# Cross attention of eight short streams in fp32, four samples side by side in four column groups of TensorE

## The chip, the cores and the metric

The kernel runs on one core of one Trainium2 chip. The metric is the device time of one execution in microseconds (us); lower is better. Engines are named as in the profile: PE is the matrix engine (PEld its weight loads), DVE, ACT and POOL are the vector, scalar and GpSimd engines, SP issues most of the DMA transfers from one queue that works strictly in order.

## The reference

One layer of a streaming encoder is computed for two groups of rows: 2048 rows of one new stream ("prompt", 16 tiles of 128 rows) and 128 rows that belong to eight running streams of 16 rows each ("samples", one tile, `S_TILE`). The change concerns the attention of the samples, in two places. Cut to these:

```python
# 1. mixer attention: the 16 rows of a sample attend to 256 cached rows and their own 16, 8 heads of 64
s = einsum("bqhd,bkhd->bhqk", q, k) * 64 ** -0.5 + bias;  att = softmax(s) @ v
y = concat(att, conv_branch) @ w_out;   x = x + rmsnorm(y) * g
# 2. cross attention: the same 16 rows attend to 256 memory rows of that sample, 4 heads of 256
q = (rmsnorm(x) @ w_mq).reshape(B, T, 4, 256)
s = einsum("bthd,bmhd->bhtm", q, mk) * 256 ** -0.5      # mk, mv = cache_mem_k, cache_mem_v
o = einsum("bhtm,bmhd->bthd", softmax(s), mv).reshape(B, T, 1024)
x = x + rmsnorm(o @ w_mo) * g
```

The caches `cache_att_k`, `cache_att_v`, `cache_mem_k` and `cache_mem_v` are inputs of the layer. A function `layout` on the host reorders inputs into the arrays that the kernel reads.

## The kernel before, in words

Stages follow one another: memory keys of the prompt, input projection and convolution (to about 640 us), band attention (`attention`, 640 to 920 us), output projection (`mixout`, 920 to 1190 us), cross attention of the prompt (`phase_cross`), the gated feed-forward layer (`gate_up`) and its down projection (`down`). Dense products use a three-product split: each fp32 operand is taken as a high and a low part in a reduced format that PE reads in one pass (tiles `sbr`, `sbx` hold these), and `mm3` / `mm3h` (lines 283 to 291) multiply high by high, high by low, low by high. A few products are left in plain fp32; the trace shows one of these as two records.

`attention` runs 128 units (8 heads by 16 row tiles), and in each head the eight-step generator `sample(s)` is woven in for one sample. It loads 256 cached keys with the key index on the partitions (`kc`, 512 KB), turns them with eight transposes on PE (line 812) through PSUM and two ACT copies (line 813) into `kt` (channel on the partitions), adds the 16 new keys (POOL, line 816), and makes the scores with four fp32 products of 32 weight columns each (line 826). Each of the four writes its own 32 rows of PSUM, that is, its own quarter of the columns of PE; in `kt` 272 columns pass. Line 845 does the same with the values.

`mixout` multiplies 17 row tiles (the samples' first) with `w_out`: 48 products of 512 columns for each (line 291). From the third tile on, after each second of the eight k-steps, `RATE` steps of the generator `cross_sample` are woven in; what is left runs after the last tile. `cross_sample` does the samples' cross attention: the query product (`dense`), 16 steps of scores, softmax, 16 steps of values, the output product (`dense`). A step of scores takes half of one sample's keys: eight transposes (line 1175), a split into high and low by ACT (1177) and DVE (1178), then eight products of 256 columns with 128 weight columns (line 1194), in which only the 16 columns of that sample are not zero; hence the two zeroed tiles `pads`, which POOL fills with a sample's 16 columns and blanks again (line 1130). A step of values splits a loaded block and has eight such products (line 1231). Cached blocks of 512 KB come into three buffers `wf`, one SP transfer each (line 1096).

The order in which each engine's instructions stand is fixed when the program is built: a scheduler places the generators' instructions by its own estimate of when they can run. So a change of steps also changes the order around them. Tile memory is laid out by hand in `Region`; a load into a buffer waits until the buffer's last reader is done.

Of the kernel before, what the change touches and what calls it, by code (L numbers as in the profile page):

```python
# [8 lines left out]
F32 = mybir.dt.float32  # L9
F32R = mybir.dt.float32r  # L10
# [24 lines left out]
RATE = 1.0  # L35
# [101 lines left out]
class Build:  # L137
# [611 lines left out]
    def att_pools(self):  # L749
        sbF, sbR, fa, fb = self.sbF, self.sbR, self.fa, self.fb  # L750
        self.attp = (Region().lay(sbF, 34.5, ("kc", 4, 2), ("kt", 4.25, 1), ("pp", 1.5, 1), ("vn", 2, 1))
# [31 lines left out]
    def attention(self):  # L783
# [14 lines left out]
        def sample(s):  # L798
            kc = self.t(pool, [P, 2, 512], F32, "kc", 2)
            nc.sync.dma_start(kc[:, :, :], A["cache_att_k"][s].rearrange("(b p) d -> p b d", p=P))  # L800
# [5 lines left out]
            kt = self.t(pool, [P, 4, PAST + DEC_S], F32, "kt", 1)  # L806
            for c2 in range(0, 4, 2):
                pt = self.t(ps_t, [P, 2, 2, P], F32, "t")
                for c in range(2):
                    for b in range(2):  # L810
                        cc = slice((c2 + c) * P, (c2 + c + 1) * P)
                        nc.tensor.transpose(pt[:, c, b, :], kc[:, b, cc], self.ident[:, :])
                nc.scalar.copy(kt[:, c2:c2 + 2, :PAST].rearrange("p c (b k) -> p c b k", k=P), pt[:, :, :, :])
                if c2 == 0:
                    yield
# [173 lines left out]
    def mixout(self, ctx):  # L989
        nc, A = self.nc, self.A  # L990
        sbF, sbR = self.sbF, self.sbR
        fr, ff = self.flex(ctx, (4096, F32R)), self.fa
# [7 lines left out]
                .at("kvh", 4, (sbR, [64, 80]), (fr, [8])).at("kvl", 4, (sbR, [68, 104]), (fr, [12])))  # L1000
# [73 lines left out]
    def cross_sample(self, pool, ps_so, ps_p):  # L1074
# [7 lines left out]
        pads = [self.t(pool, [P, KC, P], F32R, f"pad{i}", 1) for i in range(2)]  # L1082
        for pd in pads:
            nc.gpsimd.memset(pd[:, :, :].bitcast(F32), 0.0)
            yield
# [13 lines left out]
        def transposed(src, dst, scale=1.0):  # L1099
            th = self.t(pool, [P, KC, P], F32R, "sTh", 1)  # L1100
            tl = self.t(pool, [P, KC, P], F32R, "sTl", 1)
            for half in range(2):
                sl = slice(4 * half, 4 * half + 4)
                pt = self.t(ps_p, [P, 4, P], F32, "p")
                for k in range(4):
                    nc.tensor.transpose(pt[:, k, :], src(4 * half + k), self.ident[:, :])
                nc.scalar.activation(th[:, sl, :], pt[:, :, :], AF.Copy, scale=scale)
                nc.vector.scalar_tensor_tensor(tl[:, sl, :], pt[:, :, :], scale, th[:, sl, :].bitcast(F32),
                                               ALU.mult, ALU.subtract)
                yield  # L1110
            dst += [th, tl]

        def dense(lhs, wn, y):
            ahead = Ahead([lambda k=k: split(load(A[wn][k])[:, :]) for k in range(KC)])
# [6 lines left out]
        def places(s):  # L1121


            own = s * DEC_S
            other = (own + 64) % P
            return [slice(o, o + DEC_S) for o in (own, other)]

        def blank(s):
            for c in places(s):
                nc.gpsimd.memset(pads[s % 2][:, :, c].bitcast(F32), 0.0)  # L1130

        def pad(s, T):
            if s >= 2:
                blank(s - 2)
            for c, src in zip(places(s), T):
                nc.gpsimd.tensor_copy(pads[s % 2][:, :, c], src[:, :, s * DEC_S:(s + 1) * DEC_S])
            return pads[s % 2]

        def clear():
            for s in (DEC_B - 2, DEC_B - 1):  # L1140
                blank(s)

        def gather(dst, src, g):

            own, other = slice(g * 64, g * 64 + 64), slice(64 - g * 64, P - g * 64)
            nc.scalar.copy(dst[own], src[other])
            nc.vector.tensor_tensor(dst[own], dst[own], src[own], ALU.add)
# [9 lines left out]
        nc.scalar.activation(q[:, :], flat(y), AF.Copy, scale=1.0 / 16.0)  # L1157
# [549 lines left out]
```

## Time and profile before

| | |
|---|---|
| time, median of 3 runs | 3013.76 us (3012.63 to 3015.66) |
| the profiled execution's own time | 3012.76 us |
| its span in the trace | 3011.0 us |
| PE busy | 97% of the span, 16932 products |
| DVE, ACT, POOL busy | 71%, 45%, 46% |
| mean DMA rate | 166 GB/s |

The span is what the trace covers; 1.8 us of the execution lie around it. Rows of the profile's timeline read: start in us from the span's start, length in us, engine, line, what is written from what, shape, how many. Lengths of products overlap, since PE works on the next before the last has left it; the cost of a row in a busy stretch is therefore the distance from its start to the next row's start.

### The profile page before, as it was taken

What the parts mean: (1) busy time and instruction counts of PE and PEld (TensorE: products, weight loads), DVE (VectorE), ACT (ScalarE), POOL (GpSimd) and SP (SyncE); (2) the same over time, 40 slices, a digit from 0 to 9 for tenths busy, and PEclk for the clock granted to TensorE, in tenths of its full rate; (3) what the DMA queues carried; (4) which work ended last, traced back from release to release, by engine and by line L of the source; (5) the groups of instructions that cost most, each with busy time, mean ns of one, the idle gap of its engine ahead of it and who ended that gap; (6) DMA issues with size and microseconds to landing.
All of it is one profiled execution on the core that took longest, in us unless ns stands there. A gap on an engine that the chain in (4) does not pass through costs nothing.

```text
span 3011.0 us, 46007 instructions
## 1 busy us (share of the span) xinstructions
PE 2925.7 (97%) x16932; PEld 2676.2 (89%) x16932; DVE 2126.8 (71%) x3077; ACT 1354.8 (45%) x2726; POOL 1392.6 (46%) x1304
## 2 busy tenths in 40 slices
PE   8999999979999999999999999999999999999998
PEld 8999999968887887787888999999999999888786
DVE  6696895958885466435358888888788998556655
ACT  4545464658883344323234333433344444433433
POOL 0267495710013235235357565546555776424413
PEclk9999999989999999999999999999999999999999
DMA  8635255557744556324246333544334446756664
GB/s 305 241 112 183 92 162 161 170 153 184 191 132 164 176 194 212 109 75 137 95 151 227 119 136 117 200 156 152 133 136 157 140 144 208 253 174 209 224 198 164
DMA packets 196430, 500.09 MB, mean 166 GB/s; under 512 B 18981, under 2 KB 82989, under 8 KB 187875
## 3 DMA queue, kind: packets, MB, share of 16 engines
q1 hardware_dynamic: 185883, 461.09, 47.8%
q0 software_dynamic: 10320, 36.05, 3.1%
q8 instruction: 133, 2.18, 0.3%
q14 instruction: 94, 0.77, 0.1%
HBM read 365.97 MB, written 141.81 MB: 169 GB/s over the span
## 4 chain that ended last, share of the span: by engine, by line
PE 38%; DMA 4%; POOL 3%; issue 3%; DVE 2%; ACT 1%; SPq 0%; DVEq 0%; POOLq 0%; ACTq 0%
PE psb L285 12%; PE psb L284 12%; PE psb L283 12%; DMA sbf<-in_w_down_dram 2%; POOL sbf L1558 1%; PE psb L291 1%; DMA sbf<-x 1%; PE psb L1413 1%; DVE sbr L1619 0%; POOL sbf L340 0%; DVE sbr L1436 0%; DMA sbf<-in_w_gate_dram 0%; DMA sbf<-hn 0%; DMA hn<-sbf 0%; DVE flexb L1498 0%
## 5 line engine op out<-in xcount | busy, mean ns | idle before, releaser
L283 PE MATMUL psb<-sbr 128*128 128x384 f32 (+3 forms) x2808 | 944.3, 338 | 3.5 <-ACT sbr L319 1.1
L284 PE MATMUL psb<-sbr 128*128 128x384 f32 (+3 forms) x2356 | 807.6, 343 | 2.6 <-DVE sbr L320 2.4
L285 PE MATMUL psb<-sbr 128*128 128x512 f32 (+3 forms) x1848 | 634.3, 345 | 3.7 <-DVE sbr L1619 3.5
L283 PEld LDWEIGHTS psb<-sbr 128*128 128x128 f32 x2808 | 531.4, 190 | 33.5 <-ACT sbr L1618 2.4
L285 PE MATMUL psb<-sbr,sbx 128*128 128x384 f32 (+2 forms) x1484 | 478.3, 323 | 0.1
L284 PEld LDWEIGHTS psb<-sbr 128*128 128x128 f32 x2356 | 446.1, 189 | 29.2 <-DVE sbr L320 2.7
L285 PEld LDWEIGHTS psb<-sbr 128*128 128x128 f32 x1848 | 348.4, 189 | 33.4 <-DVE sbr L1619 6.9
L291 PE MATMUL psb<-sbr 128*128 128x512 f32 x1200 | 297.8, 397 | 4.3 <-POOL sbr L1271 1.5
L1436 DVE TENSOR_TENSOR sbr<-sbf,sbr 128x512 fp32r<-128x512 f32 x258 | 262.6, 1021 | 39.8 <-ACT sbr L1435 38.9
L1435 ACT CAST sbr<-sbf 128x512 fp32r<-128x512 f32 x258 | 159.3, 620 | 276.5 <-PE psb L284 234.6
L285 PEld LDWEIGHTS psb<-sbr,sbx 128*128 128x128 f32 x1484 | 281.4, 190 | 0.6 <-POOL sbx L278 0.4
L523 DVE SCALAR_TENSOR_TENSOR psb<-sbf,psb 128x768 f32<-128x768 f32 (+1 forms) x290 | 264.4, 912 | 6.2
L291 PEld LDWEIGHTS psb<-sbr 128*128 128x128 f32 x1200 | 223.6, 190 | 50.5 <-POOL sbr L1271 1.9
L1619 DVE TENSOR_TENSOR sbr<-sbf,sbr 128x384 fp32r<-128x384 f32 (+1 forms) x231 | 166.5, 743 | 92.6 <-ACT sbr L1618 91.3
L278 POOL TENSOR_TENSOR sbx<-sbf,sbr 128x1024 fp32r<-128x1024 f32 x60 | 152.9, 2551 | 81.3 <-ACT sbr L277 77.7
L1558 POOL TENSOR_TENSOR sbf<-sbf 128x512 f32<-128x512 f32 x77 | 107.6, 1401 | 167.9 <-DMA sbf<-in_w_down_dram 166.2
L1618 ACT CAST sbr<-sbf 128x384 fp32r<-128x384 f32 (+1 forms) x231 | 110.5, 497 | 164.9 <-PE psb L284 133.4
L533 POOL TENSOR_TENSOR flexb<-flexb,flexb 128x128 f32<-128x128 f32 (+1 forms) x180 | 167.1, 929 | 21.7 <-ACT flexb L532 12.1
L283 PE MATMUL psb<-sbr,sbx 128*128 128x384 f32 (+1 forms) x524 | 170.8, 327 | 2.5 <-ACT sbx L1435 1.8
L1435 ACT CAST sbx<-sbf 128x512 fp32r<-128x512 f32 x153 | 94.7, 620 | 163.4 <-PE psb L284 143.2
L1436 DVE TENSOR_TENSOR sbx<-sbf,sbx 128x512 fp32r<-128x512 f32 x153 | 154.5, 1012 | 17.9 <-ACT sbx L1435 17.5
L277 ACT CAST sbr<-sbf 128x1024 fp32r<-128x1024 f32 x98 | 102.5, 1050 | 108.2 <-PE psb L284 56.1
(339 smaller groups left out, 6159.7 us busy)
## 6 DMA issues: line engine op xcount, KB each, us to landing
af<-flexb SPq DMA_DIRECT2D x33, 1344.0 KB, 6.1
sbf<-in_w_down_dram SPq DMA_DIRECT2D x154, 256.0 KB, 3.8
sbf<-af SPq DMA_DIRECT2D x90, 384.0 KB, 3.9
sbf<-in_w_gate_dram SPq DMA_DIRECT2D x66, 512.0 KB, 3.4
sbf<-in_w_up_dram SPq DMA_DIRECT2D x66, 512.0 KB, 3.5
sbf<-x SPq DMA_DIRECT2D x49, 512.0 KB, 4.0
sbf<-in_w_in_dram SPq DMA_DIRECT2D x48, 512.0 KB, 4.2
sbr<-ks SPq DMA_DIRECT2D x28, 512.0 KB, 10.3
```

Source lines behind the costliest of these rows:

```text
L278: self.lo_engine.tensor_tensor(lo[:, :], wf[:, :], hi[:, :].bitcast(F32), ALU.subtract)
L283: nc.tensor.matmul(ps, lh, rh, start=start, stop=False, **kw)
L284: nc.tensor.matmul(ps, lh, rl, start=False, stop=False, **kw)
L285: nc.tensor.matmul(ps, ll, rh, start=False, stop=stop, **kw)
L291: nc.tensor.matmul(y[o], l, r[:, o * 512:(o + 1) * 512], start=start and x == 0, stop=stop and x == 2)
L523: nc.vector.scalar_tensor_tensor(acc if w < CW - 1 else o, src(w), cwt[:, j, w:w + 1], acc, ALU.mult, ALU.add)
L533: nc.gpsimd.tensor_tensor(o, o, v, ALU.add)
L1435: nc.scalar.copy(hs[j][:, :], src[j])
L1436: nc.vector.tensor_tensor(ls[j][:, :], src[j], hs[j][:, :].bitcast(F32), ALU.subtract)
L1558: nc.gpsimd.tensor_tensor(acc[:, :], acc[:, :], q[:, :], ALU.add if s > 0 else ALU.subtract)
L1618: nc.scalar.copy(ch[:, m], a[:, x, m])
L1619: nc.vector.tensor_tensor(cl[:, m], a[:, x, m], ch[:, m].bitcast(F32), ALU.subtract)
```

## The change

The host stores the cached keys with the channel first: `cache_att_kt` (per sample, channel by key) and `cache_mem_kt`, and `cache_mem_v` in blocks, each holding one key block or channel block of four samples side by side. In the mixer attention `kt` is loaded as it is used, into two buffers. In the cross attention, scores and values become fp32 products of 32 weight columns: block by block, four products, one for each of four samples, write four different groups of 32 rows in PSUM. `pads` now has, for each of two rounds of four samples, 32 columns for a sample, of which 16 are zero; both are zeroed once. Sixteen blocks are loaded for the scores and sixteen for the values, into five buffers. The split of the cached blocks, the transposes of the keys, the moving of `pads` and the gathering of rows go away. `RATE` is 0.85, and `cross_sample` now has 46 yields where it had 64. In `dense` weights are loaded and split one step ahead, with two pairs of split buffers for three.

```diff
-RATE = 1.0
+RATE = 0.85
...
         def sample(s):
-            kc = self.t(pool, [P, 2, 512], F32, "kc", 2)
-            nc.sync.dma_start(kc[:, :, :], A["cache_att_k"][s].rearrange("(b p) d -> p b d", p=P))
+            kt = self.t(pool, [P, 4, PAST + DEC_S], F32, "kt", 2)
+            nc.sync.dma_start(kt[:, :, :PAST], A["cache_att_kt"][s].rearrange("p (c k) -> p c k", k=PAST))
...
-            kt = self.t(pool, [P, 4, PAST + DEC_S], F32, "kt", 1)
-            for c2 in range(0, 4, 2):
-                pt = self.t(ps_t, [P, 2, 2, P], F32, "t")
-                for c in range(2):
-                    for b in range(2):
-                        cc = slice((c2 + c) * P, (c2 + c + 1) * P)
-                        nc.tensor.transpose(pt[:, c, b, :], kc[:, b, cc], self.ident[:, :])
-                nc.scalar.copy(kt[:, c2:c2 + 2, :PAST].rearrange("p c (b k) -> p c b k", k=P), pt[:, :, :, :])
-                if c2 == 0:
-                    yield
...
-                .at("kvh", 4, (sbR, [64, 80]), (fr, [8])).at("kvl", 4, (sbR, [68, 104]), (fr, [12])))
+                .at("kvh", 4, (sbR, [64, 80])).at("kvl", 4, (sbR, [68, 104]))
+                .at("kv", 4, (fr, [8, 12]), (sbF, [34.5, 38.5, 42.5])))
...
-        pads = [self.t(pool, [P, KC, P], F32R, f"pad{i}", 1) for i in range(2)]
+        pads = [self.t(pool, [P, KC, 4, 2 * DEC_S], F32, f"pad{i}", 1) for i in range(2)]
...
+        def pad(src, view, scale):
+            for half in range(2):
+                pt = self.t(ps_p, [P, 4, P], F32, "p")
+                for k in range(4):
+                    nc.tensor.transpose(pt[:, k, :], src(4 * half + k), self.ident[:, :])
+                for r in range(2):
+                    nc.scalar.activation(pads[r][:, 4 * half:4 * half + 4, :, r * DEC_S:(r + 1) * DEC_S],
+                                         view(pt, r), AF.Copy, scale=scale)
+                yield
...
+        def cached(name, x):
+            kv = self.t(pool, [P, 4, NM], F32, "kv")
+            nc.sync.dma_start(kv[:, :, :].rearrange("p a b -> p (a b)"), A[name][x])
+            return kv
+
+        def products(name, out):
+            ahead = Ahead([lambda x=x: cached(name, x) for x in range(16)], 4)
+            yield
+            for r in range(2):
+                for h_ in range(MH):
+                    for c in range(2):
+                        kv = next(ahead)
+                        for j in range(4):
+                            rows = slice(32 * j, 32 * j + 32)
+                            nc.tensor.matmul(out[rows, h_, :], pads[r][:, 2 * h_ + c, j, :], kv[:, j, :],
+                                             start=r == 0 and h_ % 2 == 0 and c == 0,
+                                             stop=r == 1 and h_ % 2 == 1 and c == 1, skip_group_check=True)
+                    yield
...
-        for x, (s, half) in enumerate(jobs):
-            kh, kl = next(ahead)
...
-            for k in range(4):
-                kk = 4 * half + k
-                for y, r in enumerate((kh, kl)):
-                    nc.tensor.matmul(sc[:, kk // 2, :], cur[:, kk, :], r[:, k, :],
...
+        sc = self.t(ps_so, [P, MH, NM], F32, "so")
+        yield from products("cache_mem_kt", sc)
...
+        o = self.t(ps_so, [P, MH, NM], F32, "so")
+        yield from products("cache_mem_v", o)
```

How the order moves, at three places. On PE in `mixout`, in the middle of the scores, the order before is the following; L1175 are transposes of cached keys, L1194 the scores, L291 the output projection and `dense`, L1015 a small product that spreads row sums.

```order
L1175 MATMUL psb<-ident_73,sbf 128x128 x8
L1194 MATMUL psb<-sbr,flexb_8748 128x256 x7
L291 MATMUL psb<-sbr,sbx 128x512 x6
L1175 MATMUL psb<-ident_73,sbf 128x128 x4
L291 MATMUL psb<-sbr,sbx 128x512 x5
L1194 MATMUL psb<-sbr,flexb_8748 128x256
L291 MATMUL psb<-sbr,sbx 128x512 x4
L1015 MATMUL psb<-sbr 128x128 x4
```

Now the same place begins as follows; L1156 are the new products, `flexb_8668` is where `pads` and two of the five `kv` buffers lie, L960 and L1006 are what L970 and L1015 were.

```order
L291 MATMUL psb<-sbr 128x512 x12
L1156 MATMUL psb<-flexb_8668 32x256
L960 MATMUL psb<-ident_73,sbr 16x128
L1156 MATMUL psb<-flexb_8668 32x256 x7
L291 MATMUL psb<-sbr 128x512 x30
L1156 MATMUL psb<-sbf,flexb_8668 32x256 x8
L291 MATMUL psb<-sbr,sbx 128x512 x6
L1006 MATMUL psb<-sbr 128x128 x4
L291 MATMUL psb<-sbr,sbx 128x512 x6
L1156 MATMUL psb<-sbf,flexb_8668 32x256 x4
L1156 MATMUL psb<-flexb_8668 32x256 x4
```

The transposes are gone, and the 128 new products stand in 22 clumps between the others; four of the 32 blocks are cut in two by other work, as the first block is here.

On PE in `attention`, the second sample before (L812 transposes of keys, L826 the scores of the sample, the rest is the prompt's attention):

```order
L866 MATMUL psb<-sbr 128x256 x2
L812 MATMUL psb<-ident_73,sbf 128x128 x4
L826 MATMUL psb<-sbf,flexb_153 32x272 x2
L883 MATMUL psb<-ident_73,flexb_153 128x128 x4
L866 MATMUL psb<-sbr 128x384 x2
L866 MATMUL psb<-sbr 128x256 x2
L896 MATMUL psb<-sbx,sbr 128x512 x2
L896 MATMUL psb<-sbx,sbr 128x384 x2
L896 MATMUL psb<-sbx,sbr 128x256 x2
L896 MATMUL psb<-sbx,sbr 128x128 x2
L883 MATMUL psb<-ident_73,flexb_153 128x128 x4
L826 MATMUL psb<-sbf,flexb_153 32x272 x2
```

and now, where L816 is what L826 was, and L856, L873 and L886 what L866, L883 and L896 were:

```order
L856 MATMUL psb<-sbr 128x384 x2
L856 MATMUL psb<-sbr 128x256 x2
L816 MATMUL psb<-sbf,flexb_153 32x272 x4
L856 MATMUL psb<-sbr 128x256 x2
L873 MATMUL psb<-ident_73,flexb_153 128x128 x8
```

Before, six of the eight samples had their four score products in two pairs that were apart; now all eight have them together.

On SP at the start of `mixout` (L1008 and L1045, now L999 and L1036, are loads of the convolution's result and of x; L1096, now L1086, loads of weights; L273 the last block of `w_out`), before:

```order
L1096 DMA sbf<-in_w_mq_dram 128x1024
L273 DMA sbf<-in_w_out_dram 128x1024
L1008 DMA flexb_153<-cs_20_92 128x512
L1008 DMA flexb_153<-cs_22_94 128x512
L1045 DMA flexb_153<-in_x_sample_dram 128x1024
```

and now:

```order
L273 DMA sbf<-in_w_out_dram 128x1024
L1144 DMA flexb_8668<-in_cache_mem_kt_dram 128x1024 x2
L999 DMA flexb_153<-cs_20_92 128x512
L999 DMA flexb_153<-cs_22_94 128x512
L1036 DMA flexb_153<-in_x_sample_dram 128x1024
```

Two blocks of cached keys now stand ahead of three loads that the first row tiles need. From the first values of `phase_cross` to the end, PE's order is the same as before.

More of the change, by code (lines that the diff above doesn't have):

```diff
@@ L1119, in dense @@
                 yield
[L1121 to L1147, printed above, removed]
         col = lambda x: lambda k: x[:, k * P:(k + 1) * P]
```

98 lines of the change are left out of this document (27 added, 71 removed).

## The prediction

> **What bounds the kernel now.** First the page: who is busy, and who ends the chain of waits.
>
> ```profile
> PE 2925.7 (97%) x16932; PEld 2676.2 (89%) x16932; DVE 2126.8 (71%) x3077; ACT 1354.8 (45%) x2726; POOL 1392.6 (46%) x1304
> PE 38%; DMA 4%; POOL 3%; issue 3%; DVE 2%; ACT 1%; SPq 0%; DVEq 0%; POOLq 0%; ACTq 0%
> ```
>
> PE is busy 97% of the span and has nine times the chain's share of any other engine. An average doesn't say that PE ends the two stages that the change touches, so I cut these out next. The columns are span, then busy time of PE, PEld, DVE, ACT, POOL, granted PE clock, DMA share, GB/s.
>
> ```profile
> 640.00:680.00 40.00, 27.93 (x160) 21.39 (x158) 21.51 (x56) 23.29 (x65) 2.61 (x7) 0.83 0.81 206
> 680.00:896.00 216.00, 208.99 (x1577) 182.30 (x1577) 178.48 (x438) 187.24 (x441) 19.46 (x29) 1.00 0.69 177
> ...
> 960.00:1160.00 200.00, 200.00 (x1088) 167.98 (x1087) 114.51 (x156) 82.98 (x158) 73.23 (x121) 1.00 0.58 192
> ```
>
> From 960 to 1160, where the samples' cross attention is woven into the output projection, PE never rests, at full clock, while DVE and ACT are at 57% and 41%. There PE work removed is time removed. In band attention PE has 209 of 216 us, but ACT 187 and DVE 178, so not all that PE saves there need come out. In the first 40 us PE waits a third of the time: nothing there is worth its full price.
>
> **The change part by part.** I price PE work by the distance from a row's start to the next row's start, in the PE timeline.
>
> ```profile
> 943.94 5.60 PE L291 MATMUL psb<-sbr 128*128 128x512 f32 x24
> 949.38 0.27 PE L970 MATMUL psb<-ident,sbr 128*16 128x128 f32 x1
> ...
> 1004.68 0.60 PE L1175 MATMUL psb<-ident,sbf 128*128 128x128 f32 x4
> 1005.03 4.15 PE L291 MATMUL psb<-sbr 128*128 128x512 f32 x17
> ...
> 1110.49 1.12 PE L1231 MATMUL psb<-flexb 128*128 128x256 f32 x8
> 1111.45 1.55 PE L291 MATMUL psb<-sbr 128*128 128x512 f32 x6
> 1112.93 0.66 PE L1015 MATMUL psb<-sbr 16*128 16x128 f32 x4
> ```
>
> So one product of 512 columns costs 5.44 / 24 = 0.227 us, four transposes 0.35, eight split products of 256 columns 0.96, that is 0.12 each. Before the product that uses only 16 rows of PE, six of 512 columns take 1.48 for 6 x 0.227 = 1.36: entering another shape costs 0.12.
>
> Removed in `mixout`: 16 steps of 8 transposes are 32 fours, 32 x 0.35 = 11.2 us; 2 x 16 steps of 8 products are 256 x 0.12 = 30.7. Together 41.9 us of PE, all of it in the stretch without rest.
>
> Added there: 128 fp32 products of 32 weight columns. The nearest rows are the samples' products in band attention (lines 826 and 845), which use the same column groups.
>
> ```profile
> 678.42 0.64 PE L845 MATMUL psb<-flexb,sbf 128*32 128x128 f32 x16
> 678.99 0.66 PE L883 MATMUL psb<-ident,flexb 128*128 128x128 f32 x4
> 679.58 0.42 PE L845 MATMUL psb<-sbf 16*32 16x128 f32 x8
> 679.93 0.86 PE L866 MATMUL psb<-sbr 128*128 128x384 f32 x4
> ...
> 759.83 0.67 PE L826 MATMUL psb<-sbf,flexb 128*32 128x272 f32 x8
> 760.42 0.66 PE L883 MATMUL psb<-ident,flexb 128*128 128x128 f32 x4
> ...
> 884.21 0.65 PE L826 MATMUL psb<-sbf,flexb 128*32 128x272 f32 x4
> 884.79 0.66 PE L883 MATMUL psb<-ident,flexb 128*128 128x128 f32 x4
> 885.38 0.65 PE L826 MATMUL psb<-sbf,flexb 128*32 128x272 f32 x4
> 885.96 0.85 PE L866 MATMUL psb<-sbr 128*128 128x384 f32 x4
> ```
>
> One fp32 product is two records. Eight records of 272 columns (four products) take 0.59, and four records (two products) 0.58: the four run beside each other, and a pair costs as much as a four. Eight records of 128 columns take 0.35, sixteen 0.57, so one pass of all four groups costs (0.57 - 0.35) / 2 = 0.11 for 128 columns, 0.22 for 256, and 0.35 - 2 x 0.11 = 0.13 is left for the way out of the shape. With the way in, a clump costs 0.25 besides its passes. The new order has 32 blocks, four cut in two, hence 36 x 2 x 0.22 = 15.8, and 22 clumps, 22 x 0.25 = 5.5: 21.3 us. `mixout` gains 41.9 - 21.3 = 20.6 us.
>
> Here a page of the Trainium skill speaks against the change: "TensorE: Matmul & The Clock Gate", section "Measured speedup vs the span model", gives 2.38 times for three column tiles, less than three. Taken over to four at the same share (3.17, an estimate from that page) the passes would cost 15.8 x 4 / 3.17 = 19.9, and the forecast below would be 2990. The rows above differ from it, 0.59 for four against 0.58 for two, and they decide.
>
> Also off PE: the split of 32 blocks on ACT and DVE, and POOL's filling and blanking of `pads`. I cost them at nothing, since PE hides them from 960 to 1160; were PE to wait there, they would be a gain more. The same count of transposes feeds `pads` as fed the split before; a softmax stands between the products as before.
>
> Band attention loses 16 x 4 transposes of keys (16 x 0.35 = 5.6 us) and puts the six halved score groups together: six times 0.58 + 0.12 - 0.01, 4.1 us. ACT loses 16 copies.
>
> ```profile
> L813 ACT COPY sbf<-psb x16: 565/586/624, 656.1 to 884.0; 128x512 f32<-128x512 f32 x16
> PE psb L866 <- DVE flexb L793: 10.0, 12, 5.1
> PE psb L812 <- ACT sbf L813: 3.3, 1, 3.3
> ```
>
> That is 16 x 0.586 = 9.4 us less on ACT, the engine next to PE, but none on DVE, for which the prompt's scores (L866) wait 10 us in all. Ends: 0, if DVE takes over, and 13, if the one wait of 3.3 for ACT goes as well. I take 8 of 9.7, since PE has 97% of most of this stage.
>
> The new waits. Products of `mixout` now read blocks straight as they land, with the output projection queued behind them on PE, so a late block stops PE; before, three buffers and the split tiles lay between.
>
> ```profile
> sbf<-in_cache_mem_k_dram SPq DMA_DIRECT2D x16, 512.0 KB, 4.6
> ...
> flexb<-in_cache_att_v_dram SPq DMA_DIRECT2D x8, 512.0 KB, 8.5
> SPq L1045 <- POOL flexb L1067: 35.5, 11, 5.6
> SPq L1008 <- DVE sbr L1024: 32.6, 7, 10.8
> ```
>
> In the new order 126 products of 512 columns stand among the scores, so 16 blocks last about 126 x 0.227 + 18 x 0.44 + 11 x 0.25 + 1 = 40 us, 2.5 each; with five buffers a buffer has 12.5 us to be filled. Landing takes 4.6, and SP may be held in front of it by a load of x (5.6 at most) or of the convolution's result (10.8 at most, 4.7 on average). 4.6 + 5.6 fits; 4.6 + 10.8 is late by 2.9. About six row tiles pass, each with one such load: ends 0 and 6 x 2.9 = 17, I take 2, the worst case about once. The rate itself fits: 0.58 busy at 192 GB/s is 331 at full, and 30 blocks and six tiles' 1.3 MB in 90 us are 260.
>
> The two blocks moved ahead of the first loads of `mixout` are 1 MB, 3.2 us at 331 GB/s. I take 0: the loads behind them waited for PE themselves before. Ends 0 and 3.2. In band attention `kt` is used two generator steps after its load is issued, four units of 216 / 112 = 1.9 us, 7.7 us; it landed in 4.9 as `kc`, the values' load in 8.5, late by 0.8 at worst, eight times: 0 to 6, taken 0.
>
> The end of `mixout`: before, 65 steps at 1.0 with 60 turns left five of `dense` for after the loop, 30 products, 6.8 us, beside the first work of the next stage. Now 47 steps at 0.85 need 55 turns, and nothing is left.
>
> ```profile
> 1192.04 1.19 PE L291 MATMUL psb<-flexb,sbx 128*128 128x512 f32 x4 [0.76 <-DVE flexb L1091]
> 1196.48 1.67 PE L318 MATMUL psb<-ident,sbf 128*128 128x128 f32 x8 [3.25 <-DVE sbr L320]
> ...
> 1207.12 6.45 PE L291 MATMUL psb<-sbr 128*128 128x512 f32 x27 [1.52 <-POOL sbr L1271]
> ```
>
> These waits, 5.5 us, may go, or, without the 6.8 us of filling, grow. Ends -5.5 and +6.8; I take 0.
>
> The sum: 20.6 + 8 - 2 = 26.6 us less than this execution's 3012.76, which is 1.0 below the median of the runs: 2986 for an execution like this one.
>
> **The rivals.** First, blocks come late more often than once: the mechanism of the new wait at its far end, 17 us, gives 2986 + 15 = 3001. For it speaks that SP was held 68 us in all in the stage's two kinds of load, against it the 12.5 us of each buffer. Chance 0.17.
>
> Second, and on the other side: every buffer's round trip fails. If landing slows to the values' 8.5 and SP's worst 10.8 comes before each round, 19.3 - 12.5 = 6.8 late, 32 / 5 = 6.4 rounds, 44 us: 2986 - 2 + 44 = 3028. It decides when the blocks' mean lateness passes 28.6 / 32 = 0.9 us. Against it: 0.58 DMA share. Chance 0.04.
>
> Third, the four groups don't overlap at full width (256 columns read from one buffer each): four times the passes, 15.8 x 3 = 47 more, 3033. The rows of line 826 speak plainly against it. Chance 0.02.
>
> Fourth, the ends add up the good way: attention 13 and the stage's end 5.5 give 2986 - 5 - 5.5 = 2975. For it: the 3.3 us wait on ACT goes with its cause. Chance 0.15.
>
> **How the numbers follow.** 0.62 is left for the sum within about 7 us, the split of the attention term and the stage's end. A measurement of this kernel can tell 0.2%, 6 us, from no change, so faster means below 3007.7. The first, the fourth and the forecast lie below it; of the first rival a tail reaches no change: 0.03. Slower is the second and third, 0.06. The range leaves out the far side of both: 2974 to 3001.
>
> **What would show it.** In the new trace line 1156 has 256 records, each four about 0.22 apart from the next four, and the row after a clump of sixteen records comes about 1.0 us after it. No line of transposes of cached keys remains, ACT's 16 copies are gone. The stretch from the first to the last `w_out` product is about 20 us shorter, without waits on PE for the cached blocks' DMA over 3 us in all; attention ends about 8 us sooner; from `phase_cross` on all rows keep their distances. I am wrong if PE waits for `kv` landings at every clump, if records of the four groups start one pass apart, or if attention keeps its length because DVE's L793 waits grow by what PE gives up.

## The result and the profile after

The changed kernel takes 2992.32 us (median of 4 runs, 2990.71 to 2996.98) against 3014.43 for the kernel before on the same chip: a ratio of 0.9924, 95% interval 0.9909 to 0.9939. The profiled execution took 2992.62, its span is 2990.8 where it was 3011.0: 20.2 us less, where 26.6 were forecast. The size of the gain is right within the range, but in part because misses cancel; the terms that missed are the interesting part.

First the page of the changed kernel, busy times of the engines and the chain's shares:

```profile
PE 2893.6 (97%) x16740; PEld 2636.6 (88%) x16740; DVE 2083.7 (70%) x3023; ACT 1314.1 (44%) x2665; POOL 1368.1 (46%) x1244
...
PE 41%; DMA 4%; POOL 3%; DVE 2%; issue 2%; ACT 0%; DVEq 0%; SPq 0%; POOLq 0%; ACTq 0%
```

PE is busy 32.1 us less (busy time contains work at a slower clock, which will matter below) and still 97% of the span, so about 12 of it came back as idle time. Where? The stretch from the first group of 24 products behind `mixout`'s first normalization to the first transposes of probabilities in `phase_cross` holds the samples' work. Its windows, before and then after; columns as in the prediction (span, busy PE, PEld, DVE, ACT, POOL, granted clock, DMA share, GB/s):

```profile
936.73:1221.80 285.07, 279.18 (x1429) 232.09 (x1429) 162.20 (x201) 116.51 (x215) 110.52 (x157) 0.99 0.57 189
```

```profile
928.70:1199.73 271.03, 260.59 (x1303) 197.04 (x1303) 112.75 (x142) 81.03 (x170) 86.18 (x97) 0.97 0.58 196
```

The stretch begins 8.0 us sooner (928.70 for 936.73), which is what attention gave. It is 14.0 us shorter: PE is busy 18.6 us less, but idles 10.4 where it idled 5.9, and its clock is 0.97 instead of 0.99. Of these 22.0 us, 1.9 are lost again behind the stretch, and 20.2 are left.

The new products look as they were priced. The PE timeline of the changed kernel, each clump with the row behind it:

```profile
1008.88 1.07 PE L1156 MATMUL psb<-sbf,flexb 128*32 128x256 f32 x16
1009.88 1.67 PE L291 MATMUL psb<-sbr,sbx 128*128 128x512 f32 x6
...
1027.58 0.64 PE L1156 MATMUL psb<-flexb 128*32 128x256 f32 x8
1028.15 1.66 PE L291 MATMUL psb<-sbr 128*128 128x512 f32 x6
...
1031.45 0.63 PE L1156 MATMUL psb<-sbf,flexb 128*32 128x256 f32 x4
1032.01 3.03 PE L291 MATMUL psb<-sbr 128*128 128x512 f32 x12
```

Sixteen records take 1.00 us to the next row, eight 0.57: four passes and two, 0.215 each, and 0.14 for leaving the shape. The four-record row is a block cut in two by the order, and it costs as much as the whole block. Next, the products' line with what its engine idled for (this is the weight loads' engine PEld; PE itself was busy without a gap from 928.70 to 1140); then the row of the waits of SP, whose queue loads the blocks; then the DMA issues with the median time to landing at the end of each row:

```profile
L1156 PE MATMUL psb<-sbf,flexb x144: 379/379/403, 1008.9 to 1088.0; 128*32 128x256 f32 x144
...
L1156 PE MATMUL psb<-flexb x112: 379/379/404, 1000.1 to 1092.8; 128*32 128x256 f32 x112
...
its engine sat idle before it (us, times) until:
  issue: 6.3, 18
```

```profile
SPq L1144 <- PE psb L1156: 54.1, 17, 6.0
```

```profile
sbf<-in_cache_mem_kt_dram SPq DMA_DIRECT2D x9, 512.0 KB, 5.2
sbf<-in_cache_mem_v_dram SPq DMA_DIRECT2D x9, 512.0 KB, 4.2
...
flexb<-in_cache_att_v_dram SPq DMA_DIRECT2D x8, 512.0 KB, 12.2
```

No product waited for a block. It is the other way round: SP waited 54 us for PE to be done with a buffer.

The loss is at the seam from `mixout` to `phase_cross`, in the same timeline:

```profile
1148.72 5.61 PE L291 MATMUL psb<-sbr 128*128 128x512 f32 x24
1154.17 1.03 PE L318 MATMUL psb<-ident,sbf 128*128 128x128 f32 x8
1160.49 8.01 PE L291 MATMUL psb<-sbr 128*128 128x512 f32 x24 [5.29 <-DVE flexb L1057]
1171.19 0.50 PE L291 MATMUL psb<-sbr 128*128 128x512 f32 x1 [2.69 <-ACT sbr L1212]
...
1173.93 20.39 PE L291 MATMUL psb<-sbr 128*128 128x512 f32 x78 [0.68 <-ACT sbr L319]
...
1199.73 1.23 PE L1245 MATMUL psb<-ident,sbf 128*128 128x128 f32 x8 [1.79 <-DVE sbf L1239]
1203.58 2.07 PE L291 MATMUL psb<-sbr 128*128 128x512 f32 x4 [2.62 <-ACT sbr L1248]
```

Read the 1160.49 row in two steps. Its 24 products are the second half of the last row tile of the output projection: with them 912 products of line 291 are done, 816 of this projection and 96 of `dense`. PE first waits 5.29 us for the DVE's scaling of the row tile before (L1057), which is what frees the PSUM that these products write. DVE in turn had waited 2.32 us for a transfer, the store of an earlier row tile:

```profile
1159.69 1.41 DVE L1057 SCALAR_TENSOR_TENSOR flexb<-psb,flexb,sbf 128x512 f32<-128x512 f32 x2 [2.32 <-DMA x<-flexb]
```

Then the 24 products take 8.01 us, where the same number take 5.61 at 1148.72: the wait is paid a second time, in a slower clock. The product at 1171.19 is the first of `phase_cross`; it waits 2.69 us for the split of its weights (L1212), and this wait too is paid again: the 78 products at 1173.93 take 20.39 us, where 78 at 0.227, and 0.17 for the last one's end, would be 17.9.

The kernel before had such a seam as well, with less of both. This is the row behind its wait of 3.25 us, 28 products in 7.79 us where 6.5 would do; then the windows of the two seams, before and after:

```profile
1197.81 7.79 PE L291 MATMUL psb<-sbr 128*128 128x512 f32 x28
```

```profile
1160.00:1221.80 61.80, 55.91 (x249) 45.15 (x247) 39.00 (x33) 27.89 (x45) 28.07 (x25) 0.97 0.58 196
```

```profile
1140.00:1199.73 59.73, 49.29 (x200) 39.30 (x198) 24.21 (x22) 20.78 (x37) 23.99 (x24) 0.89 0.50 171
```

The clock record of the trace shows where: PE's clock was half of full from 1196.8 to 1200.3 before, and now from 1158.6 to 1165.4 and from 1172.2 to 1179.1. Half of PE's busy time in these stretches is 1.7 us before and 5.5 now. So the seam costs 4.6 us more of idle time and 3.8 more of slow clock, 8.4 together.

### The profile page after: what moved, and what is told of

Same layout as the page of the kernel before. It is cut to its first block, busy times and chain, and to the rows that moved or that the text cites. A ratio compares the mean times of both kernels' runs of the same rounds, so it can differ in the third digit from the quotient of the medians.

```text
span 2990.8 us, 45392 instructions
## 1 busy us (share of the span) xinstructions
PE 2893.6 (97%) x16740; PEld 2636.6 (88%) x16740; DVE 2083.7 (70%) x3023; ACT 1314.1 (44%) x2665; POOL 1368.1 (46%) x1244
## 4 chain that ended last, share of the span: by engine, by line
PE 41%; DMA 4%; POOL 3%; DVE 2%; issue 2%; ACT 0%; DVEq 0%; SPq 0%; POOLq 0%; ACTq 0%
PE psb L285 13%; PE psb L284 13%; PE psb L283 13%; DMA sbf<-in_w_down_dram 1%; PE psb L291 1%; POOL sbf L1500 1%; DMA sbf<-x 1%; PE psb L1355 1%; DMA sbf<-hn 1%; POOL sbf L340 0%; DVE sbr L1561 0%; DMA sbf<-af 0%; DVE sbr L1378 0%; DMA hn<-sbf 0%; DVE flexb L1440 0%
## 5 line engine op out<-in xcount | busy, mean ns | idle before, releaser
L291 PE MATMUL psb<-sbr 128*128 128x512 f32 x1200 | 299.6, 401 | 14.4 <-DVE flexb L1057 5.3
L291 PEld LDWEIGHTS psb<-sbr 128*128 128x128 f32 x1200 | 227.6, 193 | 67.4 <-DVE flexb L1057 5.5
L278 POOL TENSOR_TENSOR sbx<-sbf,sbr 128x1024 fp32r<-128x1024 f32 x60 | 152.5, 2545 | 79.4 <-ACT sbr L277 75.1
L277 ACT CAST sbr<-sbf 128x1024 fp32r<-128x1024 f32 x98 | 102.4, 1049 | 103.5 <-PE psb L284 55.9
```

Source lines behind the costliest of these rows:

```text
L278: self.lo_engine.tensor_tensor(lo[:, :], wf[:, :], hi[:, :].bitcast(F32), ALU.subtract)
L291: nc.tensor.matmul(y[o], l, r[:, o * 512:(o + 1) * 512], start=start and x == 0, stop=stop and x == 2)
```

## The experiments

All ratios are against the kernel before on the same chip as the run.

**The parts alone.** `att_alone` is the kernel before with the attention part of the diff only; `cross_alone` is the changed kernel with this in place of it:

```diff
-            kt = self.t(pool, [P, 4, PAST + DEC_S], F32, "kt", 2)
-            nc.sync.dma_start(kt[:, :, :PAST], A["cache_att_kt"][s]...)
+            kc = self.t(pool, [P, 2, 512], F32, "kc", 2)
+            nc.sync.dma_start(kc[:, :, :], A["cache_att_k"][s]...)
...
+                        nc.tensor.transpose(pt[:, c, b, :], kc[:, b, cc], self.ident[:, :])
+                nc.scalar.copy(kt[:, c2:c2 + 2, :PAST]..., pt[:, :, :, :])
```

> The kernel before with one part of the change: band attention's cached keys come transposed from the host, cross attention stays as it was. Theory A (attention gives 8 to 9 us and every later row keeps its distance): 3014.4 - 8.5 = 3006, within 2; the first w_out product 8 us sooner, the first transposes of phase_cross 8 us sooner too. Rival B (what attention gains is given back at the next stage's start, since the loads and splits there set it): 3010 to 3014.

> The changed kernel with band attention's part undone: keys there are transposed on PE as before, cross attention is the new one. If the two parts add: 2992.3 + 8.5 = 3001, within 2. If attention's gain was lost at the transition to phase_cross and the whole 22 us are the cross part's: 2992 to 2995.

Measured: `att_alone` 3002.17, ratio 0.9966 (0.9954 to 0.9979); `cross_alone` 2998.68, ratio 0.9952 (0.9939 to 0.9965); before 3015.07. That is 12.9 and 16.4 us, each with an interval of some 4 us either way, and each a little more than its adding theory allowed (3004 and 2999 at the least). Both parts give, so B falls: in the trace the first product of `mixout` starts at 888.69 for 898.65, and at the first transposes of probabilities `att_alone` is 10.7 us ahead. The two together would be 29 where the whole gives 21 to 22. What the rows say of that is in the next section.

**The filling at the seam.** `fill72` sets the rate so that four steps of `dense` are left for after the loop, as there were five before:

```diff
-RATE = 0.85
+RATE = 0.72
```

> The changed kernel with RATE 0.72 instead of 0.85, so that four steps of the last dense product (24 products, 5.4 us) are left for after the loop, as five were before the change. Theory A (the loss at the end of mixout is the missing filling: 4.6 us more idle time on PE in the stretch and some 2.6 us of slow clock behind it): 2992.3 - 5 = 2987, between 2985 and 2989; the waits behind the norm's first transposes fall from 5.3 and 2.7 to under 3 in all and no group of 24 products takes over 6 us. Rival C (these waits belong to phase_cross's own loads and stand wherever the filling is): 2992, the waits the same size.

Measured: 2990.53 (2982.43 to 2993.08), ratio 0.9924. The profiled run was the fastest of the five, 2982.43, and would have proved theory A by itself; the median says 2 us. It was run again beside the unedited changed kernel.

> The changed kernel once more, unedited, on the chip on which the next three run, as their yardstick, since a profile of one run and a median of runs on another chip can't tell 5 us apart. Every theory: 2992, ratio to the kernel before 0.991 to 0.994.

> RATE 0.72 again, against the changed kernel on the same chip. In its first profile the stretch from the first w_out product to the third group of probabilities' transposes was 343.4 us against 353.1, idle time on PE 4.1 less and the granted clock behind it 0.95 against 0.90, yet the median of its runs was only 2 us below the changed kernel's. Theory A (filling is worth what that profile shows): 6 to 10 us below after_again. Theory C (the profile was a lucky run, and the gain is what idle time alone gives): 1 to 4 us below. Theory N: no difference.

Measured: `after_again` 2993.31 (2991.64 to 2995.70), ratio 0.9932; `fill72_again` 2990.31 (2982.77 to 2994.93), ratio 0.9919: 3.0 us below, in the range of theory C. All runs of each together, the changed kernel has a mean of 2993.3 over 10 and the edited one of 2989.1 over 11: 4.2 us, with a 95% interval of 3.1 either way by their scatter. These runs are from more than one chip; the six of each on the last chip alone give 4.1 us with 4.8 either way, so the size is loosely known. In the second profile of the edited kernel the seam is this:

```profile
1161.81 2.93 PE L291 MATMUL psb<-sbr,sbx 128*128 128x512 f32 x6 [4.00 <-DVE sbr L1081]
...
1170.19 0.73 PE L291 MATMUL psb<-sbr 128*128 128x512 f32 x2 [0.84 <-ACT sbr L1212]
1171.45 13.90 PE L291 MATMUL psb<-sbr 128*128 128x512 f32 x60 [0.53 <-DVE sbr L1213]
...
1191.31 1.23 PE L1245 MATMUL psb<-ident,sbf 128*128 128x128 f32 x8 [0.98 <-DVE sbf L1239]
```

The waits for L1057 and L1212 are gone or small, as A says; a new one of 4.0 us has come, for the split of `dense`'s own weights (L1081): the leftover steps stand so close behind each other that their loads and splits are late. The windows of `fill72_again`, and then of `after_again`, from the first product of `mixout` to the last row-sum product, and on to the third group of probabilities' transposes:

```profile
890.10:1126.30 236.20, 229.49 (x1218) 174.43 (x1217) 101.96 (x156) 70.36 (x161) 67.71 (x79) 0.98 0.59 198
1126.30:1236.50 110.20, 99.63 (x433) 79.89 (x432) 59.98 (x59) 44.49 (x75) 34.42 (x35) 0.94 0.46 148
```

```profile
890.52:1135.31 244.79, 238.08 (x1254) 179.36 (x1253) 111.15 (x163) 76.88 (x167) 66.64 (x79) 0.99 0.58 198
1135.31:1241.30 105.99, 90.93 (x397) 73.48 (x397) 50.34 (x52) 37.91 (x69) 30.94 (x31) 0.92 0.42 139
```

346.4 us against 350.8, although both do the same work: 4.4 us less, of which idle time in the second window makes 4.5 (10.6 for 15.1). What the first profile had on top of that, in the same windows 343.4, was luck of its run. By the medians `fill72` is 3 us faster than the changed kernel.

**RATE as it was.** The other way round: `rate100` takes the changed kernel with RATE 1.0.

> The changed kernel with the old RATE of 1.0, which undoes the diff's other part: the samples' steps then end 13 turns before the last row tile instead of five. Nothing is left for after the loop in either, so theory A (what is missing at the start of phase_cross is leftover work, not lateness) gives the same idle time in the stretch from the last row-sum product to the first probabilities' transposes, 10 to 12.5 us, and the same loss of clock; the blocks stand closer, 2.1 us each, which costs at most 2: 2992 to 2996. Rival F (what counts is how near its end the filling stops): idle time and time grow with the distance, 2997 to 3003.

Measured: 2996.26 (2991.30 to 2999.95), ratio 0.9942 (0.9928 to 0.9955). The last of the samples' products now stands at 1074.8 us instead of 1092.8, and the waits of the seam are nevertheless about as long; the one for L1057 comes a row tile sooner, with 72 products of the output projection to go instead of 24:

```profile
1150.70 8.18 PE L291 MATMUL psb<-sbr,sbx 128*128 128x512 f32 x24 [4.78 <-DVE flexb L1057]
...
1172.45 0.50 PE L291 MATMUL psb<-sbr 128*128 128x512 f32 x1 [2.69 <-ACT sbr L1212]
...
1204.82 2.08 PE L291 MATMUL psb<-sbr 128*128 128x512 f32 x4 [2.62 <-ACT sbr L1248]
```

So it is not how long before the end the filling stops. RATE 0.72 changes two things at once, though: steps stand beside the last row tiles, and four are left behind the loop. Which of the two takes the waits away no run separates. PE idles 11.1 us in the stretch from the last row-sum product, within A's 10 to 12.5. The median lies at the upper edge of A's range; 3 us above `after_again` with runs that spread over 9 is no difference that I would build on.

**What attention's gain is.** `att_copy` puts ACT's copies back, and with them the tile memory of the kernel before (a staging tile `kc`, and one buffer each for `kt` and `vn`):

```diff
-            nc.sync.dma_start(kt[:, :, :PAST], A["cache_att_kt"][s]...)
+            kc = self.t(pool, [P, 4, PAST], F32, "kc", 2)
+            nc.sync.dma_start(kc[:, :, :], A["cache_att_kt"][s]...)
...
+            for c2 in range(0, 4, 2):
+                nc.scalar.copy(kt[:, c2:c2 + 2, :PAST], kc[:, c2:c2 + 2, :])
```

> The changed kernel with ACT's 16 copies of 128x512 put back in band attention: the transposed keys land in a staging tile and are copied to kt, where the kernel before copied PE's transposes. PE's work stays as changed, and the copies stand where they stood. Theory P (the 8 to 10 us that attention gained are PE's 9.7 us of removed work): within 2 us of after_again. Theory Q (they come from the 9.4 us of ACT, the engine next to PE): 6 to 9 us above it, with new waits of PE for ACT in attention.

Measured: 2993.54, ratio 0.9934 (0.9920 to 0.9948), 0.2 us above `after_again`. By the time Q falls and P stands. The trace doesn't bear out P's reason. The last values' product of attention, 8.9 us sooner in the changed kernel (914.69 for 923.60), comes at 920.01 here, so with the copies back 5.3 of the 8.9 are gone, though PE's products are the changed kernel's. And Q's sign is there: for one line of ACT (L879) PE waits 6.5 us in all, for its counterpart in the changed kernel (L874) 0.8. The first product of `mixout` starts 3.7 us later than in `after_again`, but the waits that follow are smaller, as in its timeline

```profile
921.90 1.22 PE L291 MATMUL psb<-sbr 128*128 128x512 f32 x2 [0.93 <-ACT sbr L277]
...
932.27 5.76 PE L291 MATMUL psb<-sbr,sbx 128*128 128x512 f32 x24 [1.91 <-DVE flexb L1062]
```

against these in the changed kernel:

```profile
916.66 0.74 PE L291 MATMUL psb<-sbr 128*128 128x512 f32 x2 [1.58 <-ACT sbr L277]
...
919.79 4.07 PE L291 MATMUL psb<-sbr 128*128 128x512 f32 x10 [1.37 <-DVE sbr L278]
...
928.70 7.38 PE L291 MATMUL psb<-sbr,sbx 128*128 128x512 f32 x24 [3.58 <-DVE flexb L1057]
```

`mixout` can't start at full pace before its last weights are split (L277, L278) and its first row tile is scaled (L1057). An attention that ends sooner waits there longer: 6.5 us in the three rows of the changed kernel, 2.8 in the two of `att_copy`. At the last of these rows `att_copy` is still 3.6 us behind the changed kernel's profile (932.27 for 928.70), and at the first transposes of probabilities 2.1, where the medians show 0.2. So that attention's gain is PE's removed work alone is not shown; more than half of it hangs on the copies or on the tile memory that came with them, and the start of the next stage hides most of that.

**How the four groups share PE.** `by_sample` issues a step's eight products sample by sample:

```diff
-                    for c in range(2):
-                        kv = next(ahead)
-                        for j in range(4):
+                    kvs = [next(ahead), next(ahead)]
+                    for j in range(4):
+                        for c in range(2):
```

> The changed kernel with the eight products of a step issued sample by sample, two blocks of one sample one after the other, instead of block by block over the four samples. Same products, same blocks. Theory A (products of different column groups run beside each other, those of one group after each other, and PE issues in order): a step takes five product times of 0.44 instead of two, 2.2 instead of 0.88, 16 steps: 21 us more, 3013. Rival D (the groups run beside each other whatever the order in which they stand): 2992. Rival E (a little overlap only, from the queue of weight loads): 2996 to 3004.

> The products again sample by sample (two blocks of one sample one after the other), now with three blocks read ahead instead of four, so that each step's two blocks stand in their buffers together and the sums are the reference's. The first look at this order took as long as the changed kernel: in its trace the records stood in fours 215 ns apart as before, each four now 13 ns wide instead of 7. Theory D (each column group has its own queue and goes on by itself, so the order within a step is free): within 3 us of the changed kernel's 2993. Theory A (PE issues strictly in order, so five product times per step instead of two): 3013.

In `by_sample` a step fetched one block more than there were buffers, so that some blocks were multiplied in place of others; the number and size of products are unchanged. `by_sample_2` reads three blocks ahead. Measured: 2991.88, ratio 0.9927 (0.9913 to 0.9940), and 2994.63, ratio 0.9940 (0.9925 to 0.9955). Theory A falls, and D came. This is how a step whose two blocks lie in different buffers stands in `by_sample_2`'s instruction order:

```
L1156 MATMUL psb<-flexb_8668 32x256
L1156 MATMUL psb<-sbf,flexb_8668 32x256
L1156 MATMUL psb<-flexb_8668 32x256
L1156 MATMUL psb<-sbf,flexb_8668 32x256
... (the same for two more samples)
```

and this is how it ran:

```profile
1022.50 0.66 PE L1156 MATMUL psb<-flexb 128*32 128x256 f32 x8
1022.96 0.63 PE L1156 MATMUL psb<-sbf,flexb 128*32 128x256 f32 x8
1023.52 3.02 PE L291 MATMUL psb<-sbr,sbx 128*128 128x512 f32 x12
```

First all records of the one block, for all four samples, then all of the other: PE started them in another order than they were issued, and the step took 1.02 us to the next row. This looks as if each column group went through its own products at its own pace.

`one_group` takes the overlap away:

```diff
-                            rows = slice(32 * j, 32 * j + 32)
+                            rows = slice(32 * j, 32 * j + 32) if r == 0 and c == 0 else slice(0, 32)
```

> The changed kernel with the products of all four samples sent to the first column group, but for those of each head's first block, which stay in their four groups so that all rows are written. The samples' scores and values are thereby summed into one group: the output is left out of account, the time is not. Theory A (groups run beside each other, products of one group one after another): 28 blocks take four passes where they took one, 28 x 3 x 0.44 = 37 us more, 3030 (3020 to 3040, the lower part if the new order hides some). Rival (products of one group also overlap, or the four never did): within 5 us of 2993.

Measured: 3019.90, ratio 1.0024 (1.0013 to 1.0034): 26.6 us above `after_again`. The expectation miscounted; the first blocks of all heads in both sets of products are eight, not four, so 24 blocks and not 28 lose their overlap, 24 x 3 x 0.43 = 31. A clump of 16 records shows the price itself:

```profile
1028.03 3.64 PE L1156 MATMUL psb<-sbf,flexb 128*32 128x256 f32 x16
1031.60 1.65 PE L291 MATMUL psb<-sbr 128*128 128x512 f32 x6
```

3.57 us instead of 1.00: sixteen passes of 0.215 and the same 0.14 behind them. The overlap is whole, four for one, and without it, even with eight blocks still overlapped, the kernel is 7 us slower than the one before.

**How near the blocks are to being late.** `kv2` and `kv3` have two and three buffers instead of five:

```diff
-                .at("kv", 4, (fr, [8, 12]), (sbF, [34.5, 38.5, 42.5])))
+                .at("kv", 4, (fr, [8, 12])))
...
-            ahead = Ahead([lambda x=x: cached(name, x) for x in range(16)], 4)
+            ahead = Ahead([lambda x=x: cached(name, x) for x in range(16)], 1)
```

> The changed kernel with two buffers for cached blocks instead of five (and one block read ahead instead of four). In the changed kernel's trace the blocks landed 4.4 to 8.8 us ahead of their first product, in 3.4 to 6.9 us each. By the prediction's arithmetic (2.5 us per block, so two buffers give 5.0 from free to needed, against 4.6 to 5.2 for landing and about 1.5 for the second of a pair): each of 16 steps waits 1.5 to 2.5 us, 24 to 40 in all, 3016 to 3032, with PE waiting for the DMA in the rows of the products. Rival (the output projection woven between the steps hides it, since only the leads shrink): within 5 us of after_again.

> Three buffers for cached blocks instead of five, two blocks read ahead. With two buffers the time rose by 12 us, but PE waited for the blocks only 3.9 us and the blocks still landed 1.5 to 3.7 us ahead: the order of instructions had put the products later (the last at 1131 instead of 1093 us), more of the last dense product stood at the start of phase_cross, and the idle time there rose. Theory S (buffers act through that order): with three buffers the last product lies between 1093 and 1131 us and the time between 2993 and 3005, with under 2 us of PE waiting for blocks. Theory L (lateness itself costs): 2993, since leads of 4.4 us and more shrink by less than 5.

Measured: `kv2` 3005.25 (2999.46 to 3012.78), ratio 0.9970 (0.9957 to 0.9982), 12 us above `after_again`, between its two theories and by neither's mechanism; `kv3` 2997.59 (2997.49 to 3000.66), ratio 0.9954 (0.9938 to 0.9971), 4 us above, as theory S had it. In `kv2`:

```profile
L1156 PE MATMUL psb<-flexb x256: 379/379/404, 1000.3 to 1130.7; 128*32 128x256 f32 x128
...
  DMA flexb<-in_cache_mem_v_dram: 3.9, 2
```

PE and its weight loads waited for blocks 3.9 us in all, since the order, which is fixed when the program is built, had already put the products where it thought that blocks would be there: the last at 1130.7 us instead of 1092.8 (`kv3`: 1110.9). From the first product of `mixout` to the first transposes of probabilities PE idles 26.6 us instead of the 19.2 of `after_again`, and its clock is 0.95 for 0.98. A buffer too few shows here less as a wait for the DMA than as work moved to a place where it hides less.

## Why the prediction was right, and where not

**The samples' cross attention, 20.6 forecast.** The mechanism is as told. By the distances between rows in the trace before, the removed work was 12.0 us of transposes and 16.4 + 15.8 of products, 44.2 instead of 41.9. PE is busy 18.6 us less in the stretch, and 3.8 more of its busy time are slow clock, so the work itself fell by 22.4, and what was added is 44.2 - 22.4 = 21.8 instead of 21.3. The added side was priced right, the removed one 2.3 us too low. The record count, the pass, the 1.0 us behind a clump and the 22 clumps came as written. The row of line 826 rightly decided over the lesser speedup that the Trainium skill gives for column tiles ("TensorE: Matmul & The Clock Gate", "Measured speedup vs the span model"): `one_group` measures 3.57 for 1.00 a clump, and a pass of four groups is as long as a pass of one.

**Band attention, 8 forecast of 9.7.** Its last values' product came 8.9 us sooner (914.69 for 923.60) and `mixout`'s pace row 8.0. The size is right, but with luck: two misses cancel. These are the windows from the first scores to the first product of `w_out`, before and after:

```profile
642.07:898.65 256.58, 238.15 (x1747) 205.04 (x1747) 201.93 (x498) 211.97 (x506) 22.08 (x36) 0.97 0.70 178
```

```profile
641.18:889.85 248.67, 226.09 (x1680) 199.81 (x1680) 202.39 (x496) 204.58 (x489) 23.33 (x37) 0.95 0.72 183
```

PE's busy time fell by 12.1 us, not 9.7, and its idle time rose from 18.4 to 22.6, by 4.2 where 1.7 were allowed for. (Busy time contains waits too short for a row: with ACT's copies back, in `att_copy`, 4.9 of the 12.1 return.) Of the new idle time 3.2 us are one wait. SP held a block of `w_out` until PE was done with the samples' scores (L816, 7.0 us) and issued it at 833.0; ACT waited 4.8 us for it to split it (L277), and behind that split stood in ACT's order the copy on which the next transposes on PE depended. The wait is in `att_alone` too (3.1), and not in the kernel before. The start of `mixout` then gave 2.6 us more back (idle time to the last row-sum product 6.72 for 4.07). The prediction watched DVE's L793, for which PE waits about as long as before (10.0 us then), and not the loads of `w_out` nor L277, L278 and L1057 behind attention's end. The rows in the waits of PE after the change, with the total, the number and the longest:

```profile
PE psb L856 <- DVE flexb L793: 10.7, 7, 4.8
...
PE psb L873 <- DVE sbx L875: 3.3, 2, 3.2
```

**Late blocks, 2 forecast.** 0. The arithmetic of 12.5 us a buffer against landing and SP's holding was sound but took its worst case for granted once; the blocks whose landing the trace tells (11 of 32) were there 4.4 us or more before their first product, and with `kv3` still 1.6. The first and second rivals fell with that, and the third with `one_group`. The landings of the values in attention rose from 8.5 to 12.2 us and those of the keys from 4.9 to 8.4, and no product waited for either: the terms taken as 0 there stand, though a load of `w_out` between them did stop PE, as told above.

**The end of `mixout`, 0 forecast, ends -5.5 and +6.8.** This is the step that failed. It came out beyond the far end: idle time 4.6 us more, slow clock 3.8, together 8.4. The prediction had both facts, that five steps of filling go and that the waits there were 5.5 us, and set them against each other as if the waits might go because the work beside them went. But the rows wait for other things than that work: the last row tile needs the PSUM that L1057 frees, and `phase_cross` its split weights (L1212). Without filling these waits are 5.3 and 2.7 us. `rate100` shows them about as long when the filling ends earlier, and `fill72` that they go or shrink with filling to the end, which brings about 4 us of the 8.4 back. And the price of a wait of PE was counted once, as idle time; it is that plus the slow clock after it. A rule of the Trainium skill would have said so (same page, "Part 1: The HAM clock gate (the "warmup" mystery)": after some 3.4 us of idle PE the clock falls to half until it has been busy as long). The trace agrees: behind 5.29 us of idle time, 24 products take 2.4 us more, the same as if some ten of them ran at half speed. It asks for less, though: here the wait of 2.69 us was followed by the second stretch of half clock.

Summed by rows: -8.0 at the start of the stretch, -22.4 of work, +8.4 at the seam, -22.0 at the first transposes of probabilities. Behind them the waits for L1239 and L1248 (1.79 and 2.62 us; the latter's counterpart had been 1.10 before) bring one more stretch of half clock, 1203.0 to 1209.8, which costs 3.1 us; smaller gains leave a loss of 1.9, and 20.2 us in all. Against the forecast of 26.6 the work gave 1.8 more and the blocks cost 2 less, the seam took 8.4 and the rows behind it 1.9.

**The two parts together.** `att_alone` is 10.7 us ahead at the first transposes of probabilities, `cross_alone` 18.8 (1202.95), the whole 22.1 instead of their sum. The profiles tell where the rest is. From the start to these transposes, PE's time falls into idle time, slow clock (half of its busy time in the stretches of half clock, by the trace's clock record) and work at full clock, which is what remains. What each version has less than the kernel before, in us:

| | `att_alone` | `cross_alone` | sum | whole |
|---|---|---|---|---|
| work | 16.8 | 22.4 | 39.2 | 39.2 |
| idle time | -8.3 | -8.9 | -17.2 | -11.6 |
| slow clock | 2.2 | 5.3 | 7.6 | -5.5 |
| time | 10.7 | 18.8 | 29.6 | 22.1 |

The removed work adds up. The parts' profiles have less slow clock than even the kernel before, the whole's has more; that makes 13.1 us, more than the gap of 7.5, and idle time makes up for 5.6 of it. It is one profile of each, and the clock differs by run (see the end). But over all runs too the granted clock is 0.987 to 0.991 in the parts, 0.988 to 0.993 in the kernel before, and 0.985 to 0.987 in all but one run of the whole. By the medians the gap is 7 us with an interval about as wide. Why the whole gets less clock than its parts stays open.

## What to carry to other kernels

When a change shortens woven-in work, look at what that work was covering at the place where it used to end: its last leftover steps may have been the filling of the next stage's start-up waits, and here a rate that emptied it just before the end was some 3 to 4 us worse than one that left a few steps over. Price a wait of the matrix engine by its length and by the rows behind it, and compare two profiles by idle time, slow clock and work, not by busy time. And when loads or buffers change in a program whose order is fixed beforehand, look for the cost in where work now stands, not only in waits for the DMA.

## What was not expected of the hardware

Products of different column groups start in another order than they are issued: in `by_sample_2` the sixteen records of a step, issued sample by sample, ran block by block over all samples, at 1.02 us a step against 1.00. This order of issue cost nothing. This differs from the Trainium skill (same page, "The mechanism"), by which products start and end strictly in the order of the program; the order and rows of `by_sample_2` above are against it for column groups.

A block cut in two costs a second block: the four-record row at 1031.45 took 0.56 us to the next row, eight records 0.57.

In all fourteen traces the granted clock is either full or half, and every stretch of half clock between two of full clock lasts 3.41 us or a whole multiple of it, on a fixed grid. So what a wait costs behind it depends on where it falls: up to the last row-sum product of `mixout`, `cross_alone` idles 4.9 us and loses no clock, the whole idles 6.7 us and loses 3.3.

One profile can mislead by more than a change is worth here: `fill72`'s first profiled run was 8 us below the median of its runs, and its second one 5 us above. Between these two profiles of one program lie 12.5 us of span, of which 11.0 are slow clock and 2.0 idle time; the work is the same to 0.4.
